# A 256-column matmul made in two of 128 columns at the head of each run of 256-column products, in a Conformer/Griffin hybrid layer on one core

## The chip, the cores and the metric

The kernel runs on one core of a Trainium2 chip. The metric is the time of one execution in microseconds (us) on the device; lower is better. Profiles are one execution taken by the hardware profiler; in them PE is TensorE (the matmul engine), PEld its weight loads, DVE is VectorE, ACT is ScalarE, POOL is GpSimd and SP is SyncE, which issues most of the DMAs.

## The reference

One layer of 512 tokens and width 1024 in float32: a half-step feed-forward, a mixer, a second half-step feed-forward and a last norm.

```python
def swiglu_ffn(x, w_gate, w_up, w_down):
    return (jax.nn.silu(x @ w_gate) * (x @ w_up)) @ w_down

x = x + 0.5 * swiglu_ffn(rmsnorm(x, ffn1_norm), ffn1_w_gate, ffn1_w_up, ffn1_w_down)
x = x + hybrid_mixer(rmsnorm(x, mix_norm), w_in, ...)
x = x + 0.5 * swiglu_ffn(rmsnorm(x, ffn2_norm), ffn2_w_gate, ffn2_w_up, ffn2_w_down)
return rmsnorm(x, final_norm)
```

The hidden width of the feed-forwards is 2816. The mixer projects 1024 to 2048 columns with `w_in`, sends them in four parts of 512 through a gated causal convolution of width 31 with a layer norm and through a gated linear recurrence, and projects back with `w_out`.

## The kernel before

**Split operands.** Every matrix product keeps float32 accuracy with operands of fewer bits: each operand is a high part and a low part (`hi` is a rounded copy, `lo` is what is left), and a product is hi x hi + hi x lo + lo x hi. So each tile of a product costs three matmuls. Weights come by DMA as `raw` tiles of 128 x 1024; ScalarE makes `hi` (lines 203 and 238) and VectorE makes `lo` (line 212).

**Two ways to make the hidden layer.** In `mm_feat` (line 300) a slab of 128 hidden features is multiplied with `n` tokens: 3 x 8 matmuls whose stationary operand is a 128 x 128 block of the slab and whose moving operand is `n` token columns of the normed input `h_hi` or `h_lo`. With `n` = 512 (`ALL`) a product is 24 matmuls of 512 columns; with `n` = 256 (`A` or `B`, the two halves of the tokens) it is 24 of 256. In `mm_block` (line 310) the gate and up slabs of one `j` are taken together as a 2 x 2 block matrix and multiplied with the 2 x 2 blocks of the input in seven block products in place of eight, after Strassen and Winograd; each of the seven is 12 matmuls (3 x 4) of 256 columns, on sums and differences that are made on VectorE (`block_hi` for the weights, `quarters` and `sums` for the input, which end in the `sx` tiles S1 to S4).

**The order of the feed-forward.** There are 22 slab pairs `j` in groups of 8, 8 and 6. Pairs 0 and 1 are made early by `early_units`, on the first half of the tokens while the second half is still being normed, then on the second half: products of 256 columns. In feed-forward 1 pair 2 is made with 512 columns (`PLAIN[0]` is 3), and pairs 3 to 21 by seven products each (`seven_units`, line 452); in feed-forward 2 pairs 2 to 21 (`PLAIN[1]` is 2). Each of the first two groups is followed by `down_a_units`, whose matmuls (`mm_tok`, lines 519 to 522) have 512 columns, and the third by `down_b_units` or, in feed-forward 2, `final`, also of 512 columns. The seven products of a pair are named B11, T1, T2, B21, B22, T3 and T4; T4 of one pair is put behind the second product of the next (`late` in `ffn`, line 941), and that of a group's last pair behind the first unit of the down projection. So the matmuls of one group form a run of 256-column matmuls without a break, and the runs of pairs 3 to 7 (or 2 to 7), 8 to 15 and 16 to 21 stand between stretches of 512-column matmuls.

**The input projection.** `zc_units` (line 599) makes the convolution's gate and value channels by `mm_feat`, for channel blocks 0 and 1 in two halves of the tokens (256 columns), then everything else with 512. `transposed` (line 343) turns the normed tokens by TensorE (line 348, 128 columns each) between them.

**The order on the engines** is worked out when the program is built: units are issued in the order of the lists, and a scheduler may move single instructions of an engine by their priorities. Each matmul instruction comes with a weight load of its own, also where two matmuls in a row use the same stationary block.

The lines that the change touches are the inner loops of `mm_feat` and `mm_block`, and the callers that hand them a new argument: `ffn_units` (420), `seven_units` (452), `early_units` (514), `zc_units` (599) and `ffn` (941).

Of the kernel before, what the change touches and what calls it, by code (L numbers as in the profile page):

```python
# [13 lines left out]
P = 128  # L14
D = 1024
KT = 8
# [6 lines left out]
HT = 256  # L23
# [4 lines left out]
PLAIN = (3, 2)  # L28
BESIDE = (4, 5, 6, 9, 11, 13, 15, 18, 20)
ASIDE = 16  # L30
TAPS = 31
PR_NORM = 800
PR_CONV = -50
# [9 lines left out]
A, B, ALL = (0, HT), (HT, HT), (0, T)  # L43
# [29 lines left out]
def layer_kernel(ctx: ExitStack, tc, x, gains, w_g1, w_u1, w_d1a, w_d1b, w_in,  # L73
# [223 lines left out]
            yield 1  # L297


    def mm_feat(ps, s, t0, n):  # L300
        hi = s.hi.rearrange("p (k f) -> p k f", k=KT)
        lo = s.lo.rearrange("p (k f) -> p k f", k=KT)
        for i, (w, h) in enumerate(((hi, h_hi), (hi, h_lo), (lo, h_hi))):
            for k in range(KT):
                PE.matmul(ps, w[:, k, :], h[:, k, t0:t0 + n],  # L305
                          start=(i == 0 and k == 0), stop=(i == 2 and k == KT - 1))

    def mm_block(ps, b, a, first):  # L310
        (whi, wlo), (hhi, hlo) = b, a
        for i, (w, h) in enumerate(((whi, hhi), (whi, hlo), (wlo, hhi))):
            for k in range(4):
                PE.matmul(ps[:, 0:HT], w[:, k * P:(k + 1) * P], h[:, k, :],  # L314
                          start=(first and i == 0 and k == 0), stop=(i == 2 and k == 3),
                          skip_group_check=not first)

    pinned = [False]

# [97 lines left out]
            self[j] = slot([P, 2, T], "act", F32R)  # L417
            return self[j]

    def ffn_units(acts, j, g, u_, parts):  # L420
        off = ASIDE if len(parts) == 2 else 0
        sg_, su_ = Slab(g, off=off), Slab(u_, off=off)
        box = {}

        def product(key, s, t0, n):
            box[key] = bank("p" + key)
            mm_feat(box[key][:, :n], s, t0, n)

        def gate_out(t0, n):
            box["s"] = sp.tile([P, T], F32, name=nm("sg"), tag="sg", bufs=2)  # L430
            S.activation(box["s"][:, :n], box["gate"][:, :n], AF.Silu)

        def up_out(t0, n):
            s, a = box["s"], acts[j]
            V.tensor_mul(s[:, :n], box["up"][:, :n], s[:, :n])
            S.copy(a[:, 0, t0:t0 + n], s[:, :n])
            V.tensor_sub(a[:, 1, t0:t0 + n], s[:, :n], a[:, 0, t0:t0 + n].bitcast(F32))
            dve(0.8 if n == 256 else 1.3)

        out_ = []  # L440
        for t0, n in parts:
            us = 5.44 * n / 512
            out_.append(Unit([sg_], us, lambda t0=t0, n=n: product("gate", sg_, t0, n),
                             lambda t0=t0, n=n: gate_out(t0, n), n == T))
            out_.append(Unit([su_], us, lambda t0=t0, n=n: product("up", su_, t0, n),
                             lambda t0=t0, n=n: up_out(t0, n), n == T))
        return out_
# [1 line left out]

    def seven_units(acts, j, g, u_, q):
        pair = {"gate": g, "up": u_}
        bg, bt, b2, bt2 = (Block(pair, k) for k in ("g", "t12", "b22", "t34"))
        right = {"B11": (bg, 0), "B21": (bg, 1), "T1": (bt, 0), "T2": (bt, 1), "B22": (b2, 0),
                 "T3": (bt2, 0), "T4": (bt2, 1)}
        box = {}
        h0, h1 = slice(0, HT), slice(HT, T)

        def product(to, b, a, first):  # L460
            if first:
                box[to] = bank("p" + to)
            blk, i = right[b]
            sl = slice(i * HALF, (i + 1) * HALF)
            mm_block(box[to], (blk.hi[:, sl], blk.lo[:, sl]), q[a], first)

        def evac(to, fn):
            with tc.high_priority(offset=PR_OUT):
                fn(box[to][:, 0:HT])

        def m1(ps):
            box["s"] = sp.tile([P, T], F32, name=nm("sg"), tag="sg", bufs=2)
            S.copy(box["s"][:, h0], ps)

        def m5(ps):
            box["m"] = sp.tile([P, T], F32, name=nm("um"), tag="um", bufs=2)
            S.copy(box["m"][:, h1], ps)

        def u2(ps):
            S.copy(box["m"][:, h0], ps)  # L480

        def c11(ps):
            V.tensor_add(box["s"][:, h0], ps, box["s"][:, h0])
            S.activation(box["s"][:, h0], box["s"][:, h0], AF.Silu)
            dve(0.42)

        def c12(ps):
            V.tensor_add(box["m"][:, h0], ps, box["m"][:, h0])
            dve(0.42)

        def c22(ps):
            V.tensor_add(box["m"][:, h1], ps, box["m"][:, h1])  # L492
            dve(0.42)

        def c21(ps):
            s, a = box["s"], acts[j]
            S.activation(s[:, h1], ps, AF.Silu)  # L497
            V.tensor_mul(s, s, box["m"])  # L498
            S.copy(a[:, 0, :], s)
            V.tensor_sub(a[:, 1, :], s, a[:, 0, :].bitcast(F32))  # L500
            dve(1.4)

        units = []
        for to, b, a, first, fn in (("x", "B11", "A11", True, m1), ("z", "T1", "S1", True, m5),
                                    ("x", "T2", "S2", False, u2), ("w", "B21", "A12", True, c11),
                                    ("z", "B22", "S4", False, c12), ("x", "T3", "S3", False, c22),
                                    ("x", "T4", "A22", False, c21)):
            units.append(Unit([right[b][0]], 1.41,
                              lambda to=to, b=b, a=a, first=first: product(to, b, a, first),
                              lambda to=to, fn=fn: evac(to, fn)))  # L510
        return units


    def early_units(acts, wg, wu, between):
        e = [ffn_units(acts, j, wg[j], wu[j], [A, B]) for j in range(2)]
        return e[0][:2] + e[1][:2] + between + e[0][2:] + e[1][2:]


# [80 lines left out]
    def zc_units(c, parts):  # L599
        off = ASIDE if len(parts) == 2 else 0  # L600
        sgt, sv = Slab(split=ws_in[4 + c], off=off), Slab(split=ws_in[c], off=off)
        box = {}

        def product(key, s, t0, n):
            box[key] = bank("pz")
            mm_feat(box[key][:, :n], s, t0, n)

        def gate_out(n):
            box["s"] = sp.tile([P, T], F32, name=nm("sgc"), tag="sg", bufs=2)
            S.activation(box["s"][:, :n], box["g"][:, :n], AF.Sigmoid)  # L610

        def val_out(t0, n):
            V.tensor_mul(mx["ub"][:, c, 30 + t0:30 + t0 + n], box["v"][:, :n], box["s"][:, :n])
            dve(0.7)
            if t0 + n == T:
                if c == 1:
                    pool_convs.append(conv_pool(c))
                else:
                    convs.append(conv_dve(c))

        out_ = []
        for t0, n in parts:
            us = 5.44 * n / 512
            out_.append(Unit([sgt], us, lambda t0=t0, n=n: product("g", sgt, t0, n),
                             lambda n=n: gate_out(n)))
            out_.append(Unit([sv], us, lambda t0=t0, n=n: product("v", sv, t0, n),
                             lambda t0=t0, n=n: val_out(t0, n)))
        return out_
# [312 lines left out]
    def ffn(a0, wg, wu, wd, q, plain, between=()):  # L941
        us, late, acts = [], [], [a0] + [Acts() for _ in GROUPS[1:]]
        js = iter(range(FT))

        def put(more, n):
            us.extend(more[:n] + late + more[n:])
            late.clear()

        ready = False
        for gi, n in enumerate(GROUPS):  # L950
            for i in range(n):
                j = next(js)
                if j < 2:
                    continue
                if j < plain:
                    put(ffn_units(acts[gi], i, wg[j], wu[j], [ALL]), 1)
                    continue
                if not ready:
                    us.extend(wait(q["name"]))
                    ready = True  # L960
                m = seven_units(acts[gi], i, wg[j], wu[j], q)
                m[4].aside = j in BESIDE
                if j == FT - 1:
                    put([m[k] for k in (0, 1, 2, 3, 5, 4, 6)], 1)
                else:
                    put(m[:6], 2)
                    late.append(m[6])
            if gi < 2:
                put(down_a_units(wd[gi], acts[gi], n), 1)
            if gi == 0:  # L970
                us.extend(between)
        assert not late
        return us, acts[2]
# [127 lines left out]
```

## Time and profile before

| | us |
|---|---|
| median of three timed runs | 871.55 |
| lowest and highest | 870.31 and 871.9 |
| the profiled execution's own time | 874.41 |
| its span, first to last instruction | 872.4 |

The span runs from the first instruction of the execution to the last, and the execution's own time has a little more around it. The parts of the page that are used below: busy time by engine; the span in 40 slices with the granted TensorE clock (PEclk, tenths of full speed); groups of instructions, with count, busy time and mean duration of one. Of the trace's other views, the waits list who waited for whom; the chain of waits follows the work that ended last, in order of time, as start, length and what ran; the timeline gives an engine's instructions in order of time, equal neighbours merged with their count; and the windows give the busy time of each engine in a stretch. A matmul's own duration is longer than its distance from the next, since matmuls overlap. Times in the chain and in the timeline are us from the span's start.

### The profile page before, as it was taken

How to read it: one execution, taken by the hardware profiler on the slowest of the kernel's cores; microseconds unless marked ns; L12 is line 12 of the kernel's file. 1: busy time of each engine (PE TensorE's matmuls, PEld its weight loads, DVE VectorE, ACT ScalarE, POOL GpSimd, SP SyncE). 2: the span in 40 equal slices, each digit the busy share in tenths (PEclk: the TensorE clock that was granted, in tenths of full speed). 3: DMA queues.
4: the chain of work that ended last, by engine and by line, in shares of the span. 5: the costliest groups of instructions: out<-in, count | busy, mean ns of one | idle time of the engine just before them, and what ended most of it. 6: DMA issues, size and time to landing. Idle time of an engine off the chain costs nothing.

```text
span 872.4 us, 13745 instructions
## 1 busy us (share of the span) xinstructions
PE 849.3 (97%) x5568; PEld 772.7 (89%) x5568; DVE 638.0 (73%) x899; ACT 425.6 (49%) x677; POOL 89.6 (10%) x112
## 2 busy tenths in 40 slices
PE   7999999999999999999996999999999999999996
PEld 5999988999889998998783889999889999899985
DVE  5989765997668984569897669796547994558844
ACT  7656533556435652435742545555225654135633
POOL 2000010000110000209820010000000000000001
PEclk9999999999999999999997999999999999999999
DMA  7536895555885569655451021234312335223312
GB/s 283 150 138 241 286 323 212 179 184 171 293 308 196 191 234 369 218 201 185 146 193 48 26 72 51 96 121 125 120 49 95 111 110 166 74 73 98 104 43 96
DMA packets 36721, 139.12 MB, mean 159 GB/s; under 512 B 5041, under 2 KB 5169, under 8 KB 33970
## 3 DMA queue, kind: packets, MB, share of 16 engines
q1 hardware_dynamic: 29170, 112.04, 38.3%
q0 software_dynamic: 6912, 25.17, 7.5%
q8 instruction: 43, 0.70, 0.3%
q10 hardware_dynamic: 576, 1.05, 0.3%
q14 instruction: 20, 0.16, 0.1%
HBM read 110.98 MB, written 27.26 MB: 158 GB/s over the span
## 4 chain that ended last, share of the span: by engine, by line
PE 91%; DVE 4%; ACT 3%; DMA 1%; issue 1%; POOL 0%; SPq 0%; POOLq 0%; ACTq 0%; DVEq 0%
PE px L314 25%; PE pz L314 13%; PE pd L521 8%; PE pd L520 8%; PE pd L522 8%; PE pz L305 7%; PE pw L314 6%; PE pgate L305 3%; PE pup L305 3%; DVE pc L660 2%; PE po L520 1%; PE po L522 1%; PE po L521 1%; PE pdl L520 1%; PE pdl L521 1%; PE pdl L522 1%
## 5 line engine op out<-in xcount | busy, mean ns | idle before, releaser
L212 DVE TENSOR_TENSOR hl<-raw,hl 128x1024 fp32r<-128x1024 f32 (+1 forms) x132 | 139.9, 1063 | 45.2 <-ACT hl L203 33.1
L314 PE MATMUL px<-sx,hl 128*128 128x256 f32 x936 | 123.0, 281 | 0.0
L314 PE MATMUL pz<-sx,hl 128*128 128x256 f32 x936 | 123.0, 281 | 0.0
L212 DVE TENSOR_TENSOR hl<-tt,hl 128x1024 fp32r<-128x1024 f32 x78 | 95.0, 1218 | 35.0 <-ACT hl L238 34.9
L520 PE MATMUL pd<-hl,act 128*128 128x512 f32 x304 | 118.7, 390 | 0.0
L521 PE MATMUL pd<-hl,act 128*128 128x512 f32 x304 | 118.5, 390 | 0.0
L522 PE MATMUL pd<-hl,act 128*128 128x512 f32 x304 | 118.4, 389 | 0.0
L314 PEld LDWEIGHTS px<-sx,hl 128*128 128x128 f32 x936 | 115.8, 189 | 0.0
L314 PEld LDWEIGHTS pz<-sx,hl 128*128 128x128 f32 x936 | 115.7, 189 | 0.0
L314 PE MATMUL px<-h_hi,hl 128*128 128x256 f32 x624 | 98.7, 281 | 0.0
L238 ACT CAST hl<-tt 128x1024 fp32r<-128x1024 f32 x78 | 81.9, 1053 | 28.1 <-PE pd L522 18.4
L314 PEld LDWEIGHTS px<-h_hi,hl 128*128 128x128 f32 x624 | 84.9, 189 | 1.1 <-DVE um L492 0.4
L238 ACT CAST hl<-raw 128x1024 fp32r<-128x1024 f32 x78 | 65.2, 835 | 38.9 <-PE pd L522 30.8
L203 ACT CAST hl<-raw 128x1024 fp32r<-128x1024 f32 x54 | 56.1, 1052 | 51.7 <-PE pd L522 41.1
L522 PEld LDWEIGHTS pd<-hl,act 128*128 128x128 f32 x304 | 57.1, 188 | 11.9
L520 PEld LDWEIGHTS pd<-hl,act 128*128 128x128 f32 x304 | 57.1, 188 | 11.6
L521 PEld LDWEIGHTS pd<-hl,act 128*128 128x128 f32 x304 | 57.1, 188 | 11.3
L305 PE MATMUL pz<-h_hi,hl 128*128 128x512 f32 (+1 forms) x320 | 64.9, 352 | 0.0
L305 PEld LDWEIGHTS pz<-h_hi,hl 128*128 128x128 f32 x320 | 51.8, 188 | 9.2 <-issue 1.9
L660 DVE SCALAR_TENSOR_TENSOR pc<-sx,ch,pc 128x512 f32<-128x512 f32 x84 | 56.9, 749 | 0.0
L291 DVE TENSOR_TENSOR slo<-sraw,shi 128x1024 fp32r<-128x1024 f32 x24 | 29.3, 1222 | 29.6 <-ACT shi L290 29.5
L498 DVE TENSOR_TENSOR sg<-sg,um 128x512 f32<-128x512 f32 x39 | 27.0, 691 | 32.5 <-ACT sg L497 32.5
(181 smaller groups left out, 1348.4 us busy)
## 6 DMA issues: line engine op xcount, KB each, us to landing
raw<-in_w_g SPq DMA_DIRECT2D x44, 512.0 KB, 3.6
raw<-in_w_u SPq DMA_DIRECT2D x44, 512.0 KB, 3.6
hl<-wsi SPq DMA_DIRECT2D x16, 1024.0 KB, 4.8
sraw<-in_w_in SPq DMA_DIRECT2D x16, 512.0 KB, 6.2
wsi<-shi POOLq DMA_DIRECT2D x16, 512.0 KB, 5.9
wsi<-slo POOLq DMA_DIRECT2D x16, 512.0 KB, 5.0
raw<-in_w_d1a SPq DMA_DIRECT2D x16, 512.0 KB, 4.4
raw<-in_w_d2a SPq DMA_DIRECT2D x16, 512.0 KB, 3.5
```

Source lines behind the costliest of these rows:

```text
L203: S.copy(s.hi, s.raw)
L212: V.tensor_sub(s.lo, s.raw, s.hi.bitcast(F32))
L238: S.copy(s.hi, s.raw)
L291: V.tensor_sub(lo, raws[-1], hi.bitcast(F32))
L305: PE.matmul(ps, w[:, k, :], h[:, k, t0:t0 + n], start=(i == 0 and k == 0), stop=(i == 2 and k == KT - 1))
L314: PE.matmul(ps[:, 0:HT], w[:, k * P:(k + 1) * P], h[:, k, :], start=(first and i == 0 and k == 0), stop=(i == 2 and k == 3), skip_group_ch ...
L498: V.tensor_mul(s, s, box["m"])
L520: PE.matmul(ps, ahi, whi, start=first, stop=False)
L521: PE.matmul(ps, ahi, wlo, start=False, stop=False)
L522: PE.matmul(ps, alo, whi, start=False, stop=last)
L660: V.scalar_tensor_tensor(out=o if j == TAPS - 2 else to, in0=src, scalar=par(c, P_DW + j), in1=to, op0=ALU.mult, op1=ALU.add)
```

## The change

`mm_feat` and `mm_block` get an argument `cut`. Where it is 128, the matmul of the first of the three passes with `k` = 1, which is the second matmul of the product, is issued as two: columns 0 to 127, then 128 to 255, each with the same stationary block. All other matmuls stay whole. The argument is 128 in the first gate product of pair 0 on either half of the tokens (both feed-forwards), in the gate product of channel block 0 of the input projection on either half, and in the product B11 of the first pair of each run: pairs 3, 8 and 16 of feed-forward 1 and pairs 2, 8 and 16 of feed-forward 2.

```diff
+CUT = 128
...
+    def mm_feat(ps, s, t0, n, cut=0):
...
             for k in range(KT):
-                PE.matmul(ps, w[:, k, :], h[:, k, t0:t0 + n],
-                          start=(i == 0 and k == 0), stop=(i == 2 and k == KT - 1))
+                for c0, c1 in pieces(n, cut if i == 0 and k == 1 else 0):
+                    PE.matmul(ps[:, c0:c1], w[:, k, :], h[:, k, t0 + c0:t0 + c1],
+                              start=(i == 0 and k == 0), stop=(i == 2 and k == KT - 1))
+
+    def pieces(n, cut):
+        return ((0, cut), (cut, n)) if cut else ((0, n),)
...
+    def mm_block(ps, b, a, first, cut=0):
...
             for k in range(4):
-                PE.matmul(ps[:, 0:HT], w[:, k * P:(k + 1) * P], h[:, k, :],
-                          start=(first and i == 0 and k == 0), stop=(i == 2 and k == 3),
-                          skip_group_check=not first)
+                for c0, c1 in pieces(HT, cut if i == 0 and k == 1 else 0):
+                    PE.matmul(ps[:, c0:c1], w[:, k * P:(k + 1) * P], h[:, k, c0:c1],
+                              start=(first and i == 0 and k == 0), stop=(i == 2 and k == 3),
+                              skip_group_check=not first)
...
-            mm_feat(box[key][:, :n], s, t0, n)
+            mm_feat(box[key][:, :n], s, t0, n, cut if key == "gate" else 0)
...
-            mm_block(box[to], (blk.hi[:, sl], blk.lo[:, sl]), q[a], first)
+            mm_block(box[to], (blk.hi[:, sl], blk.lo[:, sl]), q[a], first,
+                     cut if b == "B11" else 0)
...
-        e = [ffn_units(acts, j, wg[j], wu[j], [A, B]) for j in range(2)]
+        e = [ffn_units(acts, j, wg[j], wu[j], [A, B], CUT if j == 0 else 0) for j in range(2)]
...
-            mm_feat(box[key][:, :n], s, t0, n)
+            mm_feat(box[key][:, :n], s, t0, n, CUT if key == "g" and c == 0 else 0)
...
-                m = seven_units(acts[gi], i, wg[j], wu[j], q)
+                m = seven_units(acts[gi], i, wg[j], wu[j], q, CUT if i == 0 or j == plain else 0)
```

More of the change, by code (lines that the diff above doesn't have):

```diff
@@ L297, in split_ahead @@
             yield 1
-    def mm_feat(ps, s, t0, n):
+    def mm_feat(ps, s, t0, n, cut=0):
         hi = s.hi.rearrange("p (k f) -> p k f", k=KT)
@@ L304, in mm_feat @@
             for k in range(KT):
-                PE.matmul(ps, w[:, k, :], h[:, k, t0:t0 + n],
-                          start=(i == 0 and k == 0), stop=(i == 2 and k == KT - 1))
-    def mm_block(ps, b, a, first):
+                for c0, c1 in pieces(n, cut if i == 0 and k == 1 else 0):
[4 more added lines that the diff above has]
+    def mm_block(ps, b, a, first, cut=0):
         (whi, wlo), (hhi, hlo) = b, a
@@ L418, in __missing__, with ffn_units @@
             return self[j]
-    def ffn_units(acts, j, g, u_, parts):
+    def ffn_units(acts, j, g, u_, parts, cut=0):
         off = ASIDE if len(parts) == 2 else 0
@@ L447, in ffn_units, with seven_units @@
         return out_
-    def seven_units(acts, j, g, u_, q):
+    def seven_units(acts, j, g, u_, q, cut):
         pair = {"gate": g, "up": u_}
```

## The prediction

> **What bounds the kernel now.** I read the page's first two parts and the row of the commonest matmul, then TensorE's waits.
>
> ```profile
> PE 849.3 (97%) x5568; PEld 772.7 (89%) x5568; DVE 638.0 (73%) x899; ACT 425.6 (49%) x677; POOL 89.6 (10%) x112
> PEclk9999999999999999999997999999999999999999
> ...
> L314 PE MATMUL px<-sx,hl 128*128 128x256 f32 x936 | 123.0, 281 | 0.0
> ```
>
> ```profile
> PE pm L640 <- DVE cv L664: 7.0, 1, 7.0
> ...
> PE ptr L348 <- DVE xn L334: 1.5, 1, 1.5
> ...
> PE pgate L305 <- ACT h_hi L353: 1.1, 2, 0.9
> ```
>
> TensorE is busy for 97% of the span at nearly the full granted clock, and its waits (us in total, times, longest; the longest and two of the norms are shown) lie in the start, the mixer and the norms: none of the six rows names L314, the line of the 256-column products of the feed-forwards. So in the feed-forwards the time is the number of matmuls times the distance from one start to the next. A matmul's own row (281 ns) is no help for that distance, because successive matmuls overlap. I took it from the chain of waits, where the start of one product less the start of an earlier one is divided by the matmuls between them.
>
> ```profile
> 34.97 2.72 PE pgate L305 x24
> 37.69 2.72 PE pup L305 x24
> 40.41 5.46 PE pgate L305 x24
> ...
> 144.36 1.42 PE px L314 x12
> ...
> 219.27 1.42 PE pz L314 x12
> ```
>
> From 34.97 to 40.41 there are 48 matmuls of 256 columns: 5.44 / 48 = **113.3 ns** each. From 144.36 to 219.27 there are 53 products of 12, or 636 matmuls of the same shape: 74.91 / 636 = **117.8 ns** each. So one instruction form has two paces, 4.45 ns or 4% apart. The granted clock does not explain it:
>
> ```profile
> 34.97:40.41 5.44, 5.44 (x50) 5.44 (x49) 5.01 (x7) 5.44 (x8) 0.00 (x0) 1.00 0.37 108
> 144.36:219.27 74.91, 74.91 (x638) 74.91 (x638) 1.00 0.48 164
> 154.25:164.15 9.90, 9.90 (x87) 9.90 (x86) 8.48 (x14) 6.53 (x11) 0.53 (x1) 1.00 0.36 126
> 81.00:90.89 9.89, 9.89 (x86) 9.89 (x86) 9.84 (x15) 6.62 (x11) 1.08 (x3) 1.00 0.77 274
> 568.97:578.86 9.89, 9.89 (x86) 9.89 (x86) 8.88 (x14) 5.76 (x10) 0.00 (x0) 1.00 0.34 105
> ```
>
> In these windows (length, busy time of PE, weight loads, VectorE, ScalarE, GpSimd, then clock, DMA share, GB/s; the second row counts L314 alone) the clock is 1.00 throughout. Other engines do not explain it either: the fast stretch has VectorE at 92% and ScalarE at 100%, while the slow pace is the same 9.89 us per 84 matmuls with VectorE at 8.48 or 9.84 and with DMA at 0.34 or 0.77. What differs is how a stretch was entered.
>
> ```profile
> 24.27 1.03 PE L348 MATMUL ptr<-ident,xn 128*128 128x128 f32 x8
> ...
> 29.25 0.73 PE L305 MATMUL pgate<-h_hi,hl 128*128 128x256 f32 x4 [0.24 <-ACT h_hi L353]
> ...
> 29.94 0.62 PE L305 MATMUL pgate<-h_hi,hl 128*128 128x256 f32 x4
> ...
> 104.45 0.39 PE L522 MATMUL pd<-hl,act 128*128 128x512 f32 x1
> 104.68 0.64 PE L314 MATMUL px<-h_hi,hl 128*128 128x256 f32 x4
> ...
> 325.33 0.67 PE L314 MATMUL px<-h_hi,hl 128*128 128x256 f32 x4
> ...
> 326.31 0.64 PE L314 MATMUL px<-h_hi,hl 128*128 128x256 f32 x4
> ...
> 831.67 0.67 PE L314 MATMUL px<-h_hi,hl 128*128 128x256 f32 x4
> ...
> 832.63 0.62 PE L314 MATMUL px<-h_hi,hl 128*128 128x256 f32 x4
> ```
>
> Four matmuls take 0.62 us at the quick pace and 0.64 at the slow one. After back-to-back 512-column matmuls (104.68) the pace is slow, and stays slow for hundreds of matmuls. After the eight 128-column transposes it is slow too: in the chain the products behind them (25.31, and 367.47 and 530.80 below) take 2.83 us per 24, where the quick ones above take 2.72. But where the entry was held up (a wait for ScalarE at 29.25; four matmuls in 0.67 us at 325.33 and 831.67), the pace settles quick at 29.94 and 832.63, and slow at 326.31, the same place of the other feed-forward. I read this as **two stable rhythms** of weight load and matmul, of which the steady entry always finds the slow one and a disturbed entry often the quick one. The page's matmul starts are what I have; why there are two rhythms the trace does not show.
>
> **The change part by part.** It adds twelve cuts: a matmul of 256 columns becomes two of 128, each with its own weight load (5568 loads for 5568 matmuls now; 5580 after). It removes nothing, adds no wait, no DMA, no work on another engine and no tile. So the only gain there can be is that a cut is such a disturbance.
>
> Where the cuts stand: feed-forward 1 has them at the two halves of the first early gate product and at B11 of j = 3, 8 and 16; the input projection at the two halves of its first gate product; feed-forward 2 at the two early halves and at j = 2, 8 and 16. Six stand at the head of a long run of 12-matmul products. The first feed-forward's runs have 34, 55 and 41 products (5x7, 8x7 and 6x7, less the last T4 of each, which stands apart behind 512-column matmuls), the second's 41, 55 and 41: 267 products, 3204 matmuls, and less the first three of each run 3186. At 4.45 ns each: **-14.2 us**.
>
> ```profile
> 25.31 2.83 PE pup L305 x24
> ...
> 528.31 1.30 DVE xn L334
> ...
> 529.74 1.06 PE ptr L348 x8
> 530.80 2.83 PE pgate L305 x24
> ...
> 360.94 5.66 PE pz L305 x48
> ...
> 367.47 2.83 PE pz L305 x24
> ```
>
> In feed-forward 2 the early products on the first half end in a wait for the second norm (its chain runs over VectorE and ends at L334, then the transposes), so a quicker pace there only waits longer: 0. The four on the second half run on into j = 2: 93 x 4.45 = -0.4. In the input projection 48 matmuls follow the first cut before the transposes of the next rows; those lead back to the slow pace for 24 and 24 more, until the second cut and the 96 behind it: 45 + 93 at 4.45 ns = 0.6. The mixer behind it is partly VectorE's, whose convolutions have been queued by then, so I take half: -0.3, with 0 and 0.6 as ends.
>
> The cost of a cut is not in the trace: no 128-column product is there but the transposes. They are the nearest row, 128 columns with a load each: eight in 1.03 us (24.27), less the 0.27 of the last, over seven is 109 ns. Two of these in place of one of 118 cost +0.10 us. Below, if the pieces share the time of the whole, 2 x 57 - 118 is 0; above stands the cold clock at the start:
>
> ```profile
> 14.92 4.17 PE pgate L305 x20
> ...
> L348 PE MATMUL ptr<-ident,xn x96: 270/273/474, 7.8 to 530.5; 128*128 128x128 f32 x96
> ```
>
> (the second row is the transposes' own duration, 273 ns in the middle). The first is 4.17 / 20 = 209 ns for each matmul, so +0.2 for a cut there, or +0.3 for any cut that leaves both pieces at that. I take the transposes' row: eight cuts at 0.10, one at 0.2 in the cold start, two of the projection at 0.1, and the one ahead of the norm's wait at nothing because that wait hides it: **+1.2 us**, between 0 and 3.
>
> What becomes late next: a run's preparation on VectorE. With the splitting of the input projection's weights beside it, it is busy 9.84 us per seven products (81.00), and these would take 84 x 113.3 = 9.52. Where such products follow each other (j = 4 to 6) that is 0.3 us each too much, 1 us in all; in the second run they alternate with 8.48 to 8.88 and the mean of two fits. In feed-forward 2, 8.88 fits 9.52. I put 0.3 us on it, between 0 and 1.
>
> Sum: -14.2 - 0.4 - 0.3 + 1.2 + 0.3 = **-13.4 us**. It stands against the profiled execution's 874.41 us (span 872.4 and 2.0 around it), which would become 861.0; the median of the three timed runs is 871.55, so I predict **858.2 us**.
>
> **The rivals.** *The cut is a bare cost.* The transposes are 128-column matmuls, and the stretches behind them came out slow (25.31, 367.47 and 530.80 in the chain). If a cut acts like them, no run changes pace, and the time is 871.55 + 1.2 = 872.8, or 871.6 at the lower bound. Against it: the transposes are of another form and arrive as a steady stream, and the cut makes one short disturbance. The Trainium skill, "TensorE: Matmul & The Clock Gate", section "Back-to-back issue gap", gives the spacing as a function of the columns alone (262 cycles for 256 columns, 134 for 128, an estimated 109 and 56 ns); by it a cut costs 3 ns and can bring nothing, so the time would stay at 871.6. The trace goes against that rule in so far as one shape has 113.3 and 117.8 ns here at one clock.
>
> *Some runs only.* The entry at 325 and that at 831 are one instruction sequence with two outcomes, so a cut may be a draw for each run. Runs are worth 34 to 55 x 12 x 4.45 ns = 1.8 to 2.9 us; with half of them, 871.55 - 7 + 1.2 = 865.7. The same time comes out if VectorE in feed-forward 1 stalls TensorE and the stall brings the slow pace back (half of 14.2). Also, no quick stretch of the trace reads its moving operand from the `sx` tiles, which hold four of the seven products' operands; if those force the slow pace, a run keeps it for one product and the time is the bare cost's.
>
> *The cut costs more and takes the quick stretch away.* This is the case on the slower side. Its place is the second half of the early products of feed-forward 1, quick today from 29.94 to 40.41: in the slow pace these some 90 matmuls cost +0.4. If a cut costs more than (1.74 - 0.4) / 12 = 0.11 us and no run gets quick, the kernel is slower by over 0.2%; with 0.2 each it is 871.55 + 0.4 + 2.4 = 874.4.
>
> **How the numbers follow.** Forecast (nearly all runs quick) 0.62, at 858.2, with an own range of 855.5 to 861.5: cuts at 0 give 857.0, the projection's other half 856.7, the timed runs' own spread a further 1.2; cuts at 3 and VectorE at 1 give 860.7. Some runs only 0.16, at 861.5 to 869.5. Bare cost 0.16, at 871.0 to 873.2. Slower 0.06, at 873.3 to 875. The first two hold 0.78, too little, so the range reaches into the bare cost: 855.5 to 872.0. Some 0.2% is what a measurement of this kernel can tell from no change. Faster by more than that (below 869.8): 0.62 + 0.15 = 0.77, since a win of one run is too small to see. Within it: that 0.01 and the bare cost but for its upper end, 0.16. Slower: that end and the last case, 0.07.
>
> **What would show it.** In the chain of the changed kernel: products of L314's successor at 1.36 us per 12 in place of 1.41 from the first product behind a cut to the next 512-column matmuls, in all six runs; windows of 84 matmuls of 9.52 us; the two pieces about 108 ns apart; 5580 matmuls. Right in mechanism but smaller if some runs stay at 1.41. The bare cost is shown by 1.41 everywhere. VectorE as the next bound would show as TensorE waits at that line with VectorE's line 212 behind them. The forecast is wrong above all if the steady entry behind 512-column matmuls stays as regular with the cut as without.

## The result, and the profile after

The changed kernel takes **860.66 us** (median of four runs, 860.56 to 861.62) against 871.72 us for the kernel before (four runs, 870.31 to 874.34): a ratio of 0.9872, 95% interval 0.9848 to 0.9897, or 11.1 us less. The prediction was 858.2 with a range of 855.5 to 872.0. The profiled execution of the changed kernel has a span of 858.7 us against 872.4, which is 13.7 less; why the two differences are not the same is answered by the experiments.

The page of the changed kernel: busy times, the granted clock, and two of the groups of 256-column matmuls.

```profile
PE 835.1 (97%) x5580; PEld 758.1 (88%) x5580; DVE 636.9 (74%) x899; ACT 425.1 (50%) x677; POOL 89.8 (10%) x112
PEclk9999999999999999999998999999999999999999
...
L321 PE MATMUL px<-sx,hl 128*128 128x256 f32 x936 | 118.8, 276 | 0.0
L321 PE MATMUL pz<-sx,hl 128*128 128x256 f32 x936 | 118.8, 276 | 0.0
```

There are twelve matmuls more and 14.2 us less of TensorE busy time; no other engine's work changed by more than 1.1 us, and the clock is what it was. The waits of TensorE are the same six in the same places: the largest is again `PE pm` on the convolutions, 7.1 us where it was 7.0. So nothing was hidden or uncovered; the same matmuls follow each other more closely. The chain of waits (start, length, what ran) shows it around the run of pairs 8 to 15 of feed-forward 1, first before, then after.

```profile
219.27 1.42 PE pz L314 x12
220.68 1.41 PE px L314 x12
222.09 0.23 PE pd L520
```

```profile
142.63 0.23 PE pd L530
142.85 1.50 PE px L321 x13
144.35 1.36 PE pz L321 x12
145.72 1.36 PE px L321 x12
```

```profile
215.07 1.36 PE pz L321 x12
216.44 1.36 PE px L321 x12
217.80 0.23 PE pd L528
```

Before, the run goes from 144.36 (shown in the prediction) to 222.09, 77.73 us, with 1.41 per product. After, it goes from 142.85 to 217.80, 74.95 us, and from the second product on each takes 1.36. The first has 13 matmuls and takes 1.50: that is 0.14 more than a quick product, the price of a cut. The six long runs, before and after:

| run | matmuls before | us before | us after |
|---|---|---|---|
| feed-forward 1, pairs 3 to 7 | 408 | 48.05 | 46.38 |
| pairs 8 to 15 | 660 | 77.73 | 74.94 |
| pairs 16 to 21 | 492 | 57.95 | 55.94 |
| feed-forward 2, early products from the second norm's transposes, and pairs 2 to 7 | 636 | 74.99 | 72.43 |
| pairs 8 to 15 | 660 | 77.73 | 74.94 |
| pairs 16 to 21 | 492 | 57.95 | 55.94 |
| sum | 3348 | 394.40 | 380.57 |

In the fourth row the gain of this profile is not the cut's. These products were quick before their first cut came, which is in the row of 25 matmuls:

```profile
524.25 2.73 PE pgate L308 x24
526.99 2.72 PE pup L308 x24
529.71 2.85 PE pgate L308 x25
```

The six give 13.8 us, the input projection 0.4 more (48 matmuls in 5.59 us for 5.66, 120 in 13.91 for 14.22); the rest of the span gave 0.5 back, 0.2 in the start and 0.3 behind the last runs of the two feed-forwards. VectorE stands closer behind than before:

```profile
164.00:173.52 9.52, 9.52 (x86) 9.52 (x85) 9.52 (x15) 5.69 (x10) 0.53 (x1) 1.00 0.69 242
81.00:90.52 9.52, 9.52 (x86) 9.52 (x86) 9.52 (x15) 6.64 (x11) 1.16 (x3) 1.00 0.84 297
```

In these windows of seven products (the fourth column is VectorE's busy time) it is busy for all of the 9.52 us, and TensorE still does not wait. Behind the first window VectorE has room again, 9.12 of 9.52 us in the next seven products; ahead of the second it was busy throughout in the seven products before, too.

### The profile page after: what moved, and what is told of

Same layout as the page of the kernel before. It is cut to its first block, busy times and chain, and to the rows that moved or that the text cites. A ratio compares the mean times of both kernels' runs of the same rounds, so it can differ in the third digit from the quotient of the medians.

```text
span 858.7 us, 13779 instructions
## 1 busy us (share of the span) xinstructions
PE 835.1 (97%) x5580; PEld 758.1 (88%) x5580; DVE 636.9 (74%) x899; ACT 425.1 (50%) x677; POOL 89.8 (10%) x112
## 4 chain that ended last, share of the span: by engine, by line
PE 90%; DVE 4%; ACT 3%; DMA 1%; issue 1%; POOL 0%; SPq 0%; POOLq 0%; ACTq 0%; DVEq 0%
PE px L321 25%; PE pz L321 12%; PE pd L528 8%; PE pd L529 8%; PE pd L530 8%; PE pz L308 7%; PE pw L321 6%; PE pgate L308 3%; PE pup L308 3%; DVE pc L668 2%; PE po L528 1%; PE po L530 1%; PE po L529 1%; PE pdl L528 1%; PE pdl L529 1%; PE pdl L530 1%
## 5 line engine op out<-in xcount | busy, mean ns | idle before, releaser
L321 PE MATMUL px<-sx,hl 128*128 128x256 f32 x936 | 118.8, 276 | 0.0
L321 PE MATMUL pz<-sx,hl 128*128 128x256 f32 x936 | 118.8, 276 | 0.0
L321 PEld LDWEIGHTS pz<-sx,hl 128*128 128x128 f32 x936 | 111.9, 188 | 0.0
L321 PEld LDWEIGHTS px<-sx,hl 128*128 128x128 f32 x936 | 111.9, 188 | 0.0
L308 PE MATMUL pz<-h_hi,hl 128*128 128x512 f32 (+2 forms) x322 | 64.8, 350 | 0.0
L291 ACT CAST shi<-sraw 128x1024 fp32r<-128x1024 f32 x24 | 25.3, 1053 | 48.2 <-DMA sraw<-in_w_in 19.5
```

What stands on the lines that cost most here:

```text
L291: S.copy(hi, raws[-1])
L308: PE.matmul(ps[:, c0:c1], w[:, k, :], h[:, k, t0 + c0:t0 + c1], start=(i == 0 and k == 0), stop=(i == 2 and k == KT - 1))
L321: PE.matmul(ps[:, c0:c1], w[:, k * P:(k + 1) * P], h[:, k, c0:c1], start=(first and i == 0 and k == 0), stop=(i == 2 and k == 3), skip_gro ...
```

## The experiments

The theory after the result: weight loads and 256-column matmuls have two stable rhythms, 113.3 and 117.8 ns; the entry from 512-column matmuls always finds the slow one; the cut is a disturbance that moves the run behind it to the quick one. Rivals: a rearranged order of instructions, the size or the place of the cut, the second load of the same weights, or a change that comes by itself from one execution to the next.

**The kernel before, once more** (no edit).

> The kernel before, once more. Two stable rhythms: all six long runs of the feed-forwards at 117.8 ns per matmul as in the first profile, 870 to 873 us. If the pace of a run is a new draw in every execution, one or more of the six long runs is at 113.3 ns here, and each of those takes 1.8 to 2.9 us off.

Measured: 871.01 us, ratio to the kernel before 0.9995 (0.9985 to 1.0005), as it must be. But its profiled execution took 870.79 us with a span of 868.8, and its chain shows at the second norm of feed-forward 2:

```profile
528.92 1.06 PE ptr L348 x8
529.98 2.75 PE pgate L305 x24
532.73 2.72 PE pup L305 x24
535.45 2.72 PE pgate L305 x24
```

Here the products behind the transposes take 2.72 per 24, where the first profile had 2.83 at the same place, and they keep it: these 636 matmuls take 72.19 us in place of 74.99. The five other long runs are at 117.8 ns as before. So in both profiles five entries come out slow, and this one, behind a wait, is a draw: one program, two outcomes, 2.8 us apart. The profile from which the prediction was made (874.41 us) had drawn the slow one.

**One cut only**, at pair 8 of feed-forward 1.

```diff
-                m = seven_units(acts[gi], i, wg[j], wu[j], q, CUT if i == 0 or j == plain else 0)
+                m = seven_units(acts[gi], i, wg[j], wu[j], q, CUT if j == 8 and plain == PLAIN[0] else 0)
```

(with the cuts of the early products and of the input projection taken out as well).

> One cut only, at B11 of pair 8 of feed-forward 1. If a cut sets the pace of the run behind it and nothing else, the run of pairs 8 to 15 takes 74.9 us in place of 77.7 and the other five stay at 117.8 ns: 2.8 us less than before, some 868.9 us. If the gain of the change came from a rearranged order of instructions, the five others change too, or this one does not.

Measured: 868.63 us, ratio 0.9969 (0.9956 to 0.9981). In the profiled execution pairs 8 to 15 take 74.94 us, the other two long runs of feed-forward 1 and all three of feed-forward 2 what they took in the first profile, to 0.01 us. The heads of the run of pairs 8 to 15 and of the next one, pairs 16 to 21:

```profile
144.18 1.50 PE px L321 x13
145.68 1.36 PE pz L321 x12
...
264.11 1.42 PE px L321 x12
265.52 1.41 PE pz L321 x12
```

The cut acts on the run behind it and on nothing else, and a rearranged order is out. This execution took 871.46 us, with the slow draw in feed-forward 2; the other five took 868.38 to 869.98.

**A cut at pair 2 of feed-forward 2 only.**

```diff
+                m = seven_units(acts[gi], i, wg[j], wu[j], q, CUT if j == 2 else 0)
```

> One cut only, at pair 2 of feed-forward 2. In the first profile that run was slow, in the repeat it was quick without a cut. If the repeat is the common case, the cut brings nothing in the median (871.5, with its own cost of 0.1) and only takes the executions at 874 to 875 away. If the first profile is the common case, the run of pairs 2 to 7 gains 492 times 4.45 ns or 2.2 us and the median is 869.4.

Measured: 871.49 us over twelve executions, ratio 0.9996 (0.9985 to 1.0007): nothing, as expected of a run that is commonly quick already. The slowest took 872.51, where the 29 executions of the kernel before beside it reach 874.76. The profiled one had drawn the quick rhythm ahead of the cut and kept it.

**Other sizes and places of the cut**: 64 and 192 columns, and the fourth matmul in place of the second.

```diff
-CUT = 128
+CUT = 64
```

```diff
-                for c0, c1 in pieces(HT, cut if i == 0 and k == 1 else 0):
+                for c0, c1 in pieces(HT, cut if i == 0 and k == 3 else 0):
```

> The same twelve cuts with 64 and 192 columns in place of 128 and 128. If any short matmul at the head is disturbance enough, all six runs are at 113.3 ns and the time is within 1 us of the changed kernel's 860.7. If the size decides the phase in which the two streams meet, the runs stay at 117.8 ns and the time is 871.5 to 873.

> The fourth matmul of the first pass is cut in 128 and 128, not the second. If the rhythm only has to be disturbed, the place does not matter: 860.7 within 1 us, six runs at 113.3 ns. If the cut has to come in the transition from the 512-column matmuls, where the second stands, the runs stay at 117.8 ns and the time is 871.5 to 873.

Measured: 861.49 us, ratio 0.9886 (0.9872 to 0.9901), and 861.33, ratio 0.9885 (0.9870 to 0.9899). In both all five runs behind 512-column matmuls have the lengths of the table to 0.01 us. So behind 512-column matmuls neither the size nor the second place is needed. With the cut of 64 the early products of feed-forward 2 came out slow behind the transposes:

```profile
527.50 2.83 PE pup L308 x24
530.33 2.93 PE pgate L308 x25
533.26 2.83 PE pup L308 x24
...
541.74 1.50 PE px L321 x13
543.24 1.36 PE pz L321 x12
```

Their own cut (the row of 25) left them slow, and the cut at pair 2 (the row of 13) then set the run right. The second cut of the input projection, also in a stretch behind transposes, left it slow as well: its last 120 matmuls took 14.32 us, where the cut of 128 in the same place gives 13.91. So behind transposes the size was not indifferent, in the one profile that there is of it.

**A cut at every pair**, 33 more than in the change.

```diff
-                m = seven_units(acts[gi], i, wg[j], wu[j], q, CUT if i == 0 or j == plain else 0)
+                m = seven_units(acts[gi], i, wg[j], wu[j], q, CUT)
```

> The changed kernel with a cut at B11 of every pair, 33 more. If the quick rhythm holds against a cut, each costs 0.06 to 0.14 us as measured at the heads: 862.7 to 865.3 us. If every cut is a new draw, some pairs fall back to 117.8 ns until the next pair and the time is above 866.

Measured: 865.47 us, ratio 0.9930 (0.9913 to 0.9947). That is (865.47 - 860.66) / 33 = 0.15 us for each cut by the medians; by the runs, 75.83 us with seven more cuts against 74.94, it is 0.13. The median is 0.2 us above the upper end of what I had expected. The quick rhythm holds against a cut in every one of the 33.

**An additional matmul in place of the cut**, behind the second matmul, 128 or 256 columns long. Its result goes to columns of the bank that are not read; the cuts of the early products and of the projection are out.

```diff
+                if cut and i == 0 and k == 1:
+                    PE.matmul(ps[:, HT:HT + 128], w[:, k * P:(k + 1) * P], h[:, k, 0:128],
+                              start=False, stop=False, skip_group_check=True)
```

> No matmul is cut; at the six heads an additional matmul of 128 columns follows the second, into columns of the bank that are not read; early products and input projection as before. If a short matmul is what disturbs, the six runs are at 113.3 ns: the changed kernel's 860.7 plus up to 1 us. If it takes the split of a product's own matmul, or fewer columns in all, the runs stay slow: 872 us.

> The same with an additional matmul of 256 columns, on the same weights as the one before it. It is as long as its neighbours and disturbs nothing: the runs behind 512-column matmuls stay at 117.8 ns and the time is before plus six times 0.12, 872.3 us. If one more instruction, or the same weights twice in a row, is what changes the pace, the runs are quick: 861 to 862 us.

Measured: 873.81 us, ratio 1.0029 (1.0018 to 1.0041), with 128 columns, and 872.11, ratio 1.0008 (0.9994 to 1.0021), with 256. The second is as expected: one more matmul on the same weights leaves the pace as it was. The first is a miss. I had expected one short matmul to be enough, and every run behind 512-column matmuls stayed slow. Worse, in feed-forward 2:

```profile
544.92 2.72 PE pup L308 x24
547.64 0.23 PE px L320 x2
547.87 0.06 PE px L324
547.92 1.23 PE px L320 x10
549.15 1.41 PE pz L320 x12
550.57 1.41 PE px L320 x12
```

The early products are quick (2.72), the additional matmul is the row of 0.06 at line 324, and from there on each product takes 1.41: a short matmul can also throw a quick run back.

**Two additional matmuls of 128 columns**, and **one behind the third matmul.** My second theory was that it takes two short ones in a row, as the two pieces of a cut are; the rival was that the one had come at the wrong moment.

```diff
+                if cut and i == 0 and k == 1:
+                    for e in range(2):
+                        PE.matmul(ps[:, HT + e * cut:HT + (e + 1) * cut],
+                                  w[:, k * P:(k + 1) * P], h[:, k, 0:cut],
+                                  start=False, stop=False, skip_group_check=True)
```

```diff
-                if cut and i == 0 and k == 1:
+                if cut and i == 0 and k == 2:
```

> No cut; at the six heads two additional matmuls of 128 columns in a row behind the second, into columns that are not read. If two short matmuls in a row are what brings the quick rhythm and one is not, the six runs are at 113.3 ns and the time is 861.5. If it takes the split of a product's own matmul, the runs stay at 117.8 ns: 872.5 or more.

> No cut; one additional matmul of 128 columns at the six heads, behind the third matmul instead of the second. If one short matmul never brings the quick rhythm, the runs stay slow, the first run of feed-forward 2 included: 872.5 to 875. If only the moment in the slow rhythm's cycle was wrong in the run with the extra behind the second, the runs are quick here: 861.

Measured: 863.5 us, ratio 0.9905 (0.9872 to 0.9937), for two, and 861.92, ratio 0.9887 (0.9854 to 0.9919), for one behind the third. Both bring the quick rhythm to all runs. (With two the time is 2 us above what I had expected. The profiled execution, of 863.91 us, had the slow draw in the early products of both feed-forwards, 0.4 and 0.6 us, which I had not put in; and 3.4 us of it lie outside its span of 860.5, where the changed kernel's has 2.0. The other execution, of 863.08 us, has no profile.) The second theory falls: one short matmul is enough if it stands one matmul later. Two timelines of TensorE at the same entry, the one behind the second matmul first:

```profile
144.43 0.40 PE L320 MATMUL px<-h_hi,hl 128*128 128x256 f32 x2
144.67 0.22 PE L324 MATMUL px<-h_hi,hl 128*128 128x128 f32 x1
144.73 0.45 PE L320 MATMUL px<-h_hi,hl 128*128 128x256 f32 x2
145.01 0.64 PE L320 MATMUL px<-h_lo,hl 128*128 128x256 f32 x4
145.48 0.63 PE L320 MATMUL px<-h_hi,hl 128*128 128x256 f32 x4
```

```profile
142.37 0.52 PE L320 MATMUL px<-h_hi,hl 128*128 128x256 f32 x3
142.72 0.22 PE L325 MATMUL px<-h_hi,hl 128*128 128x128 f32 x1
142.78 0.34 PE L320 MATMUL px<-h_hi,hl 128*128 128x256 f32 x1
142.95 0.64 PE L320 MATMUL px<-h_lo,hl 128*128 128x256 f32 x4
143.43 0.62 PE L320 MATMUL px<-h_hi,hl 128*128 128x256 f32 x4
```

Up to the fourth row the two look alike (four matmuls in 0.64); the last row is at 0.63 in the one, slow, and 0.62 in the other, quick. What differs is one whole matmul more ahead of the short one. What decides is when the short one comes, then, and not that it comes.

**One short matmul in the middle of a quick run**: the changed kernel with one additional matmul of 128 columns behind the second of B11 at pair 12 of feed-forward 1.

```diff
-                for c0, c1 in pieces(HT, cut if i == 0 and k == 1 else 0):
+                for c0, c1 in pieces(HT, cut if cut > 1 and i == 0 and k == 1 else 0):
...
+                if cut == 1 and i == 0 and k == 1:
+                    PE.matmul(ps[:, HT:HT + P], w[:, k * P:(k + 1) * P], h[:, k, 0:P],
+                              start=False, stop=False, skip_group_check=True)
...
-                m = seven_units(acts[gi], i, wg[j], wu[j], q, CUT if i == 0 or j == plain else 0)
+                m = seven_units(acts[gi], i, wg[j], wu[j], q, CUT if i == 0 or j == plain else int(j == 12 and plain == 3))
```

> The changed kernel with one additional matmul of 128 columns in B11 of pair 12 of feed-forward 1, in the middle of a quick run. If one short matmul throws a quick run back, as in feed-forward 2 of the run with the extra 128, pairs 8 to 11 stay at 113.3 ns and the rest, some 27 products, is at 117.8: 1.5 us more than the changed kernel, 862.2. If the quick rhythm holds, as it did against 33 cuts, the whole run is at 113.3 ns: 860.8.

Measured: 861.59 us, ratio 0.9883 (0.9851 to 0.9915), and in the chain:

```profile
177.83 1.59 PE px L321 x14
179.42 0.06 PE px L325
179.48 1.23 PE px L321 x10
180.71 1.41 PE pz L321 x12
182.12 2.83 PE px L321 x24
...
217.45 1.41 PE px L321 x12
218.87 0.23 PE pd L531
```

Quick up to the short matmul, slow from it to the end of the run: the run takes 76.53 us in place of 74.94, 1.6 longer where 1.5 was expected. The median does not show all of it (two executions, 0.9 above the changed kernel's).

**The changed kernel without the four early cuts.**

```diff
-        e = [ffn_units(acts, j, wg[j], wu[j], [A, B], CUT if j == 0 else 0) for j in range(2)]
+        e = [ffn_units(acts, j, wg[j], wu[j], [A, B]) for j in range(2)]
```

> The changed kernel without the four cuts in the early products; the two of the input projection and the six at the heads of the long runs stay. The early stretch of feed-forward 1 is quick without a cut and that of feed-forward 2 mostly, so only the cost of the cuts goes, 0.14 us each at most: 860.2 us, the same as the changed kernel within what can be told. If the early cut on the second half is what makes feed-forward 2's first run quick, that run is slow in some executions and the time is up to 2 us longer.

Measured: 860.43 us over five executions (860.33 to 860.96), ratio 0.9870 (0.9849 to 0.9891). That is 0.2 us below the changed kernel, not to be told from it: the early cuts bring nothing that can be measured. Its profile shows something else, in the last run of feed-forward 1:

```profile
308.12 4.15 PE px L321 x36
312.27 1.41 PE pz L321 x12
313.68 1.41 PE px L321 x12
```

It is quick for 35 products and falls back in the third of the first row, for the last six (56.23 us where the table has 55.94). At that place, in pair 21, the changed kernel's profile has a hold-up of some 20 ns (one distance of 131 ns between starts) and then goes on quick. The run with the matmul at pair 12 falls back at the same place of feed-forward 2 (56.23 us again). So a run can also fall back where TensorE is held up a little, and whether it does differs from profile to profile; what holds it up there no view shows.

## Why the prediction was right, and where its size was off

- *Two paces of one shape, at one clock, set by the entry.* Right, and shown: one cut moves one run (pair 8), one short matmul moves it back (pair 12), and five entries never leave 117.8 ns in any profile without a disturbance.
- *All six runs become quick, -14.2 us.* Right in mechanism for the five runs behind 512-column matmuls, which are quick behind the cut in every profile that has it. The sixth, the first of feed-forward 2, was quick ahead of its cut in the changed kernel's profile; that a cut turns it when it is slow shows only with 64 columns. The six runs of the two profiles differ by 13.8 us with the cuts counted in. But the sum was made on one execution and carried to the median, and that execution was not the common one: it had drawn the slow rhythm in the early products and pairs 2 to 7 of feed-forward 2, where the common execution is already quick (nine of the fourteen profiles are, and a cut at pair 2 alone leaves the median where it was). The mis-sized term is these (492 - 3 + 93) x 4.45 ns = 2.6 us. They are in the difference of the spans, 13.7, and not in that of the medians, 11.1. Without them the sum is -10.8. The forecast of 858.2 was 2.5 us too low for this reason. I had seen the draw at 325 and 831 and had not asked whether the entry behind the second norm, which is held up too, was one.
- *The rival that transposes show the cut's effect.* Behind the second norm they were no steady slow case, as I took them: nine of the fourteen profiles are quick there, ahead of any cut. In the input projection, where TensorE does not wait ahead of the transposes, the products behind them are slow in all fourteen until a cut comes.
- *The rival of the bare cost.* It falls with the six runs. The Trainium skill, "TensorE: Matmul & The Clock Gate", section "Back-to-back issue gap", has the table of spacings by the columns alone from which the prediction let a cut bring nothing; the section calls that table the gap of a single matmul in isolation, and says that in a stream of weight loads and matmuls both set the spacing. The runs here do not follow the table, with 74.94 and 77.73 us for the same 660 matmuls with and without one of them cut, and neither pace is the 109 ns that can be estimated from it.
- *The price of a cut, 0.10 us.* It is 0.13 to 0.15. The two pieces are 60 ns apart, not the 108 that the prediction named as a sign; the next matmul starts 109 ns later, and the one after it 172 ns later still. The row of the transposes gave the right order of size for the cost, by other distances.
- *The input projection, -0.3 before its cuts at 0.2.* It gave 0.4 with the cuts counted in, near the upper end. The mixer hid nothing of it: from the end of these products to the next early product it is 137.2 us in both profiles.
- *VectorE next, 0.3 us.* It is busy for all of some windows, and no wait of TensorE for it shows in the feed-forwards' long runs. Whether the hold-up in pair 21 is its doing is not shown.
- *The `sx` operands may force the slow pace.* They do not: the two groups shown above that read them have a mean of 276 ns in place of 281.

The rival "some runs only" is not what the change does, but its reason is real: draws were seen at entries that wait and at the hold-up in pair 21, not at entries out of a steady stream.

What stays open is why there are two rhythms. The longest weight load of the products that read `sx` was 193 ns before and is 188 after. The order is regular: in the run of pairs 8 to 15 every third load takes 192 or 193 ns before, the others 187 or 188, and behind the head of the run none is longer than 188 after. Whether that is cause or effect no run here tells. Nor was it tried at which places in the slow rhythm a short matmul works, beyond the two.

## What to carry to other kernels

Take the distance between starts, not the duration of a matmul, and compare stretches of the same shape in one trace: two values at one clock meant here that time was to be had without touching the work. A single short matmul at the right place at the head of a run was worth 4% of it, and one in the middle of a quick run lost as much of what followed; so look at the pace behind it, for each run. And before a sum is carried from one profiled execution to a median, ask which of its stretches another execution may have drawn otherwise.

## What the runs showed of the hardware that was not expected

- 256-column matmuls, each with its weight load, run at 113.3 or 117.8 ns from start to start at the full granted clock, and keep either pace over as many as 660 matmuls; 512-column ones run at 227 ns.
- One matmul of 128 columns behind the second of a run leaves it slow, behind the third makes it quick, and in the middle of a quick run makes the rest slow (76.53 us for 74.94). Two of 128 in a row at the head of a run behind 512-column matmuls made it quick at each place tried (the second matmul or the fourth cut, two more behind the second), and left quick ones quick in all 33 cuts of the run with a cut at every pair. Pieces of 64 and 192 did the same there, and left two stretches behind transposes slow.
- At the slow pace every third weight load took 192 or 193 ns in place of 188 (pairs 8 to 15 of feed-forward 1, before); at the quick pace none did.
- One program gives executions 2.8 us apart by the rhythm that a single entry behind a wait happens to find.
